# Column norms of the keys by full float32 matmuls on three column strips, keys turned on VectorE, in a hybrid RWKV-7 block

## The chip, the cores and the metric

The kernel runs on one core of a Trainium2 chip. The metric is the device time of one execution in microseconds (us). Engines are named as in the profile: PE is TensorE's matmul stream and PEld its weight loads, DVE is VectorE, ACT is ScalarE, POOL is GpSimd, and SP is the engine that issues the DMAs. Each of them works through its own queue of instructions in the order in which the program was built.

## The reference, cut to what matters

One layer of a language model with two branches that read the same normalised input (528 positions: 16 learned meta tokens and 512 of the sequence; model width 2048):

```python
P = hn @ w_in                          # 2048 -> 4*1024 + 64 + 64 + 4*1024 columns
r, k, v, g_r, wl, al = split(P[:RW])   # after a token shift
decay = exp(-exp(w_raw(wl)));  a = sigmoid(a0 + al @ a_lora_up)
kk = k * k_k;  kk = kk / max(norm(kk, per head of 64), 1e-12)
k  = k * (1 + (a - 1) * k_a)
# per head, step by step over the positions, in chunks of 64:
S = S * w_t - (S @ kk_t) (kk_t * a_t)^T + v_t k_t^T;   y_t = S @ r_t
y_a = (groupnorm(y) + bonus(r, k, v)) * silu(g_r)
y_b = Bg * causal_conv3(Cg * hc) * silu(g_c)          # the other branch
out = rmsnorm(h + concat(y_a, y_b) @ w_out)
```

What the change touches is the preparation of the recurrence: the squared norm of kk per head and position, and the two operands B (from kk * a) and K (from k) of the state's update, which the recurrence needs with the positions on the partitions.

## The kernel before

**Main stream.** The projection runs as one long stream of matmuls on PE. A tile is 128 output columns by 528 positions and takes 2048 rows of the weight as 16 steps of 128; the weight of a tile comes as four *quarters* (128 by 512, four of the 16 steps each), numbered 0 to 259 over the stream. Each product is done as three fp32r matmuls, high weight by high input, high weight by low input, low weight by high input (`steps`, L306 to L318; the matmul is L315). `prefetch` (L130 to L138) brings two quarters with one DMA `wr` on SP (L134). `split_w` (L123 to L128) then casts each quarter to its high half `wh` on ACT (L126) and subtracts to get the low half `wl` (L127), on DVE for even quarters and on POOL for odd ones. Six buffers of each are in use.

The stream visits the tiles in a fixed plan: k, r, v of the eight head pairs (two heads of 64 make one tile of 128), g (the gate), and C, h, B, gc of the other branch, by turns two pairs and one set C, h, B, gc; the last four sets come at the end. Pair 1 is in the first turn, pairs 2 and 3 in the second, and so on. When a tile is complete it is evacuated: L334 scales it from PSUM (for k, r, v, g, C, h, B, gc, each in two halves), L351 and L352 on ACT and DVE do the token shift of r and g, L362 belongs to the gate. For the other branch h is followed by a product on POOL (L401), a scaling on ACT (L403) and two steps of the convolution on DVE (L405).

**What stands between.** The preparation of a pair (`prepare`, from L569) is a function that issues its own instructions and, between them, calls `fill(ns)`, which lets the main stream issue for so many nanoseconds of counted PE time. The constants are in the table `FW` (L43 to L46). So the order of PE's queue is written by hand, by these fills. On the other engines a scheduler sets the order: it takes the instructions by priority and estimated readiness, with the weight splits 3000 and some evacuations 6000 ns ahead of the place at which they were issued (`WEIGHTS`, `AHEAD`). `later` (L482) puts a few steps on a clock of their own.

**The part changed,** per pair `i` in `prepare`:

- `sq` = (k * k_k) squared, on ACT (L615); split in high and low halves by `split` (L548 to L553: cast L551 on ACT, subtract L552 on DVE); `rk` (r times bonus factors) split likewise (L617).
- Gram blocks (`gram`, L623 to L630): for each chunk and each of the two heads one float32 matmul of 64 rows, 128 by 128. Eight chunks go in one cluster into four PSUM banks, then `masked` (L632) takes them to `gt` on DVE.
- fill gram2 (4800), then chunk 8's two Gram blocks in the banks misc and ser, and 16 transposes of B and K by PE (L655, an identity as the other operand) into two banks of the pool tz; ACT copies them to `bt` (L661).
- fill gram3 (3500), then `n2`: the norms as column sums. The weight is a column of ones for each head (`ones[:, P:P+2]`, 128 by 2), the moving operand is `sq`'s high and low half, in two pieces of 288 positions: four matmuls (L666, L667), two copies on ACT (L668). Then `zb`, two matmuls for the bonus (L670, L671) and a copy (L672).
- fill misc (2000). Then SP issues a block of DMAs: `sn` (the norms to DRAM, L685), `sg` (Gram blocks, L689), `ar` and `gt` to the operand store `opd` (L567), `d` and `nd` back (L697, L698) for the solve of 16 by 16 triangles on DVE (L701 to L734), four for `bt` (`stash`, L752 to L755), `rbd` (L758), eight for `vs` (v turned by DVE in 32 by 32 blocks, L762).

Later the inverses of pairs of preparations (`invert`, L772) and at the end the recurrence (`recur`, L875) run on PE. The recurrence loads 64 by 64 weights from the stored operands; its state update `zs` (L941) uses B and K.

Of the kernel before, what the change touches and what calls it, by code (L numbers as in the profile page):

```python
# [9 lines left out]
F32 = mybir.dt.float32  # L10
# [8 lines left out]
P = 128  # L19
# [21 lines left out]


FW = dict(  # L43
    evac=34, start=1062, lora=2200, gram=8000, gram_b=13500, gram2=4800, gram3=3500, misc=2000, v=2000, vt=1000, solve=22500, solve_first=26000,
    tr=3200, lev=3000, cp=4200, out=1500, begin=17000, p=2900, u=2900, s=5200, last=3700, mix=2600,
)  # L46

# [29 lines left out]
def hymba_kernel(ctx: ExitStack, tc: tile.TileContext, xt, xtok, w_in, w_out, pv, lup, cst, msk, gf, out):  # L77
# [84 lines left out]
    def tr(name, dt=F32):  # L162
        return cq.tile([P, LP], dt, tag="tr", name=name, bufs=5)
# [384 lines left out]
    def split(t, name, n):  # L548
        hi = tr(f"{name}_h", F32R)[:, 0:n]
        lo = tr(f"{name}_l", F32R)[:, 0:n]  # L550
        nc.scalar.copy(hi, t)  # L551
        nc.vector.tensor_tensor(out=lo, in0=t, in1=hi.bitcast(F32), op=ALU.subtract)  # L552
        return hi, lo  # L553
# [15 lines left out]
    def prepare(i):  # L569
# [43 lines left out]

        sq = tr(f"sq{i}")
        nc.scalar.activation(sq, k, AF.Square, scale=col(V_KK, i))  # L615
        sqh, sql = split(sq, f"sq{i}", LP)
        rh, rl = split(r, f"rk{i}", SEQ)  # L617
        fill(FW["gram_b" if p else "gram"])

        gt = cq.tile([P, 2, NCH, P], F32, tag=f"gt{p}", name=f"gt{i}")  # L620
        bt = cq.tile([P, 2, NCH - 1, CH], F32, tag="bt", name=f"bt{i}")

        def gram(z, c, c0):  # L623
            for h, hs, ho in heads:
# [7 lines left out]
        def masked(z, c0, c1):  # L632
            with ahead():
                for h in range(2):
                    nc.vector.tensor_tensor(
                        out=gt[:, h, c0:c1],
                        in0=z[h],
                        in1=gmask[:, h].unsqueeze(1).to_broadcast([P, c1 - c0, P]),
                        op=ALU.mult,
                    )  # L640
# [6 lines left out]
        masked(za, 0, 4)  # L647
        masked(zc, 4, 8)
        fill(FW["gram2"])
        ze = [pi.tile([P, 1, P], F32, tag=("misc", "ser")[h], name=f"g{i}_8_{h}") for h in range(2)]  # L650
        zz = [pz.tile([P, NCH - 1, CH], F32, tag="tz", name=f"bt{i}_{h}") for h in range(2)]
        gram(ze, 8, 8)
        for c in range(NCH - 1):
            for h, hs, ho in heads:
                nc.tensor.transpose(  # L655
                    zz[h][:, c], bk[hs, c, h : h + 2, :].rearrange("p a s -> p (a s)"),
                    ident[hs, 64 * h : 64 * h + 64],
                )
        masked(ze, 8, 9)
        for h in range(2):  # L660
            nc.scalar.copy(bt[:, h], zz[h])  # L661
        fill(FW["gram3"])
        n2 = tr(f"n2{i}")
        for j, (a, b) in enumerate(((0, 288), (288, LP))):
            z = pi.tile([2, b - a], F32, tag=("misc", "ser")[j], name=f"n2_{i}_{a}")
            nc.tensor.matmul(z, ones[:, P : P + 2], sqh[:, a:b], start=True, stop=False)  # L666
            nc.tensor.matmul(z, ones[:, P : P + 2], sql[:, a:b], start=False, stop=True)  # L667
            nc.scalar.copy(n2[0:2, a:b], z)  # L668
        zb = pz.tile([P, SEQ], F32, tag="tz", name=f"zb{i}")
        nc.tensor.matmul(zb, ones[:, 0:P], rh, start=True, stop=False)  # L670
        nc.tensor.matmul(zb, ones[:, 0:P], rl, start=False, stop=True)  # L671
        nc.scalar.copy(r, zb)  # L672
        fill(FW["misc"])

# [7 lines left out]
        def blocks(t):  # L682
            return bass.AP(tensor=t.tensor, offset=t.offset, ap=[[BLK, 8 * NCH], [CH, 16], [1, 16]])

        nc.sync.dma_start(  # L685
            bass.AP(tensor=sn.tensor, offset=sn.offset, ap=[[CH, 2], [P, NCH], [1, CH]]), c3(n2[0:2])
        )
        for h in range(2):
            nc.sync.dma_start(rows(sg, h), gt[64 * h : 64 * h + 64, h, :, 0:CH])  # L689
        NB = 8 * NCH  # L690
# [59 lines left out]
        later(16500 if p else 33000, load_inverse)  # L750

        for h, hs, ho in heads:  # L752
            stash(i, bt[hs, h], O_B, CH, 64 * h, 64, 0, NCH - 1)
            stash(i, bt[ho, h], O_K, CH, 64 * h, 64, 0, NCH - 1)
        until("v", i)  # L755
        v = got["v", i]
        nc.vector.tensor_tensor(out=r, in0=r, in1=v[:, CH:LP], op=ALU.mult)
# [117 lines left out]
    def recur(ch):  # L875
        ops = {}
        load_chunk(ch, 0, range(NPAIR), ops)
        load_chunk(ch, 1, range(NPAIR), ops)
        st = None
        for c in range(NCH):  # L880
            last = c == NCH - 1
            z = [pz.tile([P, 2, 4, CH], F32, tag="tz", name=f"rz{c}_{e}") for e in range(2)]
            for k in range(4):
                for part in range(0 if c else 1, 2):
                    for e in range(2):
                        t = ops[c, 2 * k + e]
                        o = O_KK if part else O_AR
                        for h, hs, ho in heads:
                            nc.tensor.matmul(  # L889
                                z[e][ho if e else hs, 0, k], t[hs, o : o + CH],  # L890
                                t[hs, O_V : O_V + CH] if part else st[hs, 4 * e + k],
                                start=(part == 0 or c == 0), stop=(part == 1),
                            )
            pn = ch.tile([P, 2, 4, CH], F32, tag="pn", name=f"pn{c}", bufs=2)
            with ahead():
                for e in range(2):
                    nc.scalar.activation(pn[:, e], z[e][:, 0], AF.Copy, scale=-1.0)
            if c and not last:
                load_chunk(ch, c + 1, range(0, 4), ops)
            fill(FW["p"])  # L900
            for k in range(4):
                for e in range(2):
                    t = ops[c, 2 * k + e]
                    for h, hs, ho in heads:
                        m = ho if e else hs
                        nc.tensor.matmul(z[e][hs, 1, k], t[m, O_X : O_X + CH], pn[m, e, k], start=True, stop=True)
            u = ch.tile([P, 2, 4, CH], F32, tag="u", name=f"u{c}", bufs=2)
            with ahead():
                nc.scalar.copy(u[:, 0], z[0][:, 1])
                nc.vector.tensor_copy(u[:, 1], z[1][:, 1])  # L910
            if c and not last:
                load_chunk(ch, c + 1, range(4, NPAIR), ops)
            fill(FW["u"])
            here, there = [], []
            if not last:
                zs = pi.tile([P, NPAIR, CH], F32, tag="misc", name=f"zs{c}")
            if c:
                zy = pi.tile([P, NPAIR - 1, CH], F32, tag="ser", name=f"zy{c}")
            for k in range(4):
                for e in range(2):  # L920
                    t, j = ops[c, 2 * k + e], 4 * e + k
                    if not last:
                        here += [(zs, j, t, O_B, u[:, e, k], 0, 2), (zs, j, t, O_K, t[:, O_V : O_V + CH], 1, 2)]
                    if c and j < NPAIR - 1:
                        there += [
                            (zy, j, st[:, j], O_AR + CH, t, 0, 3),
                            (zy, j, t[:, O_V : O_V + CH], O_KK + CH, t, 1, 3),
                            (zy, j, u[:, e, k], O_BR, t, 2, 3),
                        ]
                    elif c:  # L930

                        here += [
                            (z[0][:, 0], 0, t, O_AR + CH, st[:, j], 0, 3),
                            (z[0][:, 0], 0, t, O_KK + CH, t[:, O_V : O_V + CH], 1, 3),
                            (z[0][:, 0], 0, t, O_BR, u[:, e, k], 2, 3),
                        ]
            for n in range(max(len(here), len(there))):
                if n < len(here):
                    d, j, t, o, x, a, b = here[n]
                    for h, hs, ho in heads:  # L940
                        nc.tensor.matmul(d[hs, j], t[hs, o : o + CH], x[hs], start=(a == 0), stop=(a == b - 1))  # L941
                if n < len(there):
                    d, j, x, o, t, a, b = there[n]
                    for h, hs, ho in heads:
                        nc.tensor.matmul(d[ho, j], t[hs, o : o + CH], x[hs], start=(a == 0), stop=(a == b - 1))  # L945
            if not last:
                new = ch.tile([P, NPAIR, CH], F32, tag="st", name=f"st{c}", bufs=2)
                scale = dd[:, c].unsqueeze(2).to_broadcast([P, NPAIR, CH])
                with ahead():
                    if c:  # L950
                        nc.vector.tensor_tensor(out=new, in0=zs, in1=st, op=ALU.add)
                    nc.vector.tensor_tensor(out=new, in0=new if c else zs, in1=scale, op=ALU.mult)
                st = new
            if c:
                norm(ch, (zy, z[0][:, 0, 0:1]), c)
            fill(FW["s"])
# [278 lines left out]
```

## Time and profile before

| what | value |
|---|---|
| median of 3 runs | 1056.57 us (1055.68 to 1056.75) |
| the profiled execution | 1055.68 us, of it the span 1053.9 us |
| granted TensorE clock | 0.996 |
| PE busy | 1035.8 us, 98% of the span |
| PEld, DVE, ACT, POOL busy | 90%, 54%, 35%, 29% |
| one projection matmul, 258 or 512 columns, start to start | 0.12 us, 0.23 us |
| `wl` on DVE, alone | 0.69 us |
| `wh` on ACT | 0.62 us |
| 32 by 32 transposes of 128x512 on DVE (L785) | 0.70 us |

How to read it. The page's first part gives each engine's busy time and its share of the span; the chain is followed back from the last instruction to what released each step. The timeline lists instructions by start, with the duration as modelled; as matmuls overlap, the distance from one start to the next says more about PE than a duration does. In brackets stands how long the engine had been idle, and what ended that. The list of waits gives the total, the number and the longest.

### The profile page before, as it was taken

The page shows a single profiled execution, that of the slowest core. Times are in us where ns is not written, and L with a number is a line of the kernel's source. Part 1 is how long each engine was busy: PE and PEld are TensorE (multiplying, and loading weights), DVE is VectorE, ACT ScalarE, POOL GpSimd, SP SyncE. Part 2 cuts the span into 40 slices and gives each one's busy share as a digit, 9 for nine tenths or more (in the row PEclk, how much of TensorE's full clock was granted, in tenths as well). Part 3 has the DMA queues.
Part 4 walks back from the last instruction along what each step waited for, and adds up shares of the span by engine and source line. Part 5 has one row for each costly group of instructions (what it writes and reads, how often), then busy time and mean ns, then how long its engine had stood idle before and what let it go on. Part 6 is the DMA issues. An engine that isn't in the chain of part 4 may idle for free.

```text
span 1053.9 us, 23986 instructions
## 1 busy us (share of the span) xinstructions
PE 1035.8 (98%) x9973; PEld 945.8 (90%) x9973; DVE 565.4 (54%) x1072; ACT 366.3 (35%) x682; POOL 307.8 (29%) x315
## 2 busy tenths in 40 slices
PE   7999999999999999999999999999999999999996
PEld 6999998999998999989999989888898988888885
DVE  6774965559563658653757642455454771212132
ACT  7553422433332433233443232222222432323232
POOL 0132413324222323132323231323233242424232
PEclk9999999999999999999999999999999999999999
DMA  8446475364843363753364648777644978323314
GB/s 295 137 121 158 117 177 142 108 154 119 207 141 114 109 161 116 175 155 114 104 170 129 169 134 288 233 216 247 184 144 110 280 225 305 98 85 98 100 61 160
DMA packets 182893, 167.49 MB, mean 159 GB/s; under 512 B 120960, under 2 KB 143232, under 8 KB 182400
## 3 DMA queue, kind: packets, MB, share of 16 engines
q1 hardware_dynamic: 182208, 164.90, 54.0%
q8 instruction: 78, 1.28, 0.5%
q10 hardware_dynamic: 576, 1.07, 0.3%
q14 instruction: 31, 0.25, 0.1%
HBM read 129.05 MB, written 36.88 MB: 157 GB/s over the span
## 4 chain that ended last, share of the span: by engine, by line
PE 91%; DVE 4%; issue 2%; DMA 1%; ACT 1%; POOL 1%; SPq 0%; DVEq 0%; ACTq 0%; POOLq 0%
PE o L1070 17%; PE ps_g L315 9%; PE ps_C L315 9%; PE ps_gc L315 9%; PE ps_k L315 9%; PE ps_B L315 8%; PE ps_h L315 8%; PE ps_r L315 7%; PE ps_v L315 7%; PE g L625 2%; PE zs L941 1%; PE rz L889 1%; PE ps_lora L315 1%; PE zy L945 1%; DMA wq<-in_w_in_dram 1%
## 5 line engine op out<-in xcount | busy, mean ns | idle before, releaser
L127 POOL TENSOR_TENSOR wl<-wr,wh 128x512 fp32r<-128x512 f32 x150 | 210.4, 1405 | 458.0 <-ACT wh L126 428.0
L126 ACT CAST wh<-wr 128x512 fp32r<-128x512 f32 x312 | 188.8, 619 | 390.0 <-PE o L1070 93.6
L127 DVE TENSOR_TENSOR wl<-wr,wh 128x512 fp32r<-128x512 f32 x162 | 124.4, 773 | 244.0 <-ACT wh L126 243.6
L1070 PE MATMUL o<-wh,m 128*128 128x512 f32 (+1 forms) x484 | 145.3, 384 | 0.0
L1070 PEld LDWEIGHTS o<-wh,m 128*128 128x128 f32 x484 | 89.6, 188 | 21.3
L1070 PE MATMUL o<-wl,m 128*128 128x512 f32 (+1 forms) x242 | 92.6, 389 | 0.0
L315 PE MATMUL ps_k<-xl,wh 128*128 128x264 f32 x256 | 73.1, 286 | 0.0
L315 PE MATMUL ps_v<-xh,wh 128*128 128x264 f32 x256 | 73.1, 286 | 0.0
L315 PE MATMUL ps_g<-xh,wl 128*128 128x258 f32 (+1 forms) x256 | 72.2, 282 | 0.9 <-DVE wl L127 0.8
L315 PE MATMUL ps_r<-xh,wh 128*128 128x258 f32 (+1 forms) x256 | 72.2, 282 | 0.8 <-ACT wh L225 0.8
L315 PE MATMUL ps_k<-xh,wh 128*128 128x264 f32 x256 | 73.0, 285 | 0.0
L315 PE MATMUL ps_h<-xh,wl 128*128 128x258 f32 (+1 forms) x256 | 72.8, 284 | 0.0
L315 PE MATMUL ps_k<-xh,wl 128*128 128x264 f32 x256 | 72.7, 284 | 0.0
L315 PE MATMUL ps_v<-xh,wl 128*128 128x264 f32 x256 | 72.7, 284 | 0.0
L315 PE MATMUL ps_v<-xl,wh 128*128 128x264 f32 x256 | 72.7, 284 | 0.0
L315 PE MATMUL ps_g<-xl,wh 128*128 128x258 f32 (+1 forms) x256 | 72.5, 283 | 0.0
L315 PE MATMUL ps_h<-xh,wh 128*128 128x258 f32 (+1 forms) x256 | 72.3, 282 | 0.0
L315 PE MATMUL ps_C<-xh,wh 128*128 128x258 f32 (+1 forms) x256 | 72.3, 282 | 0.0
L315 PE MATMUL ps_g<-xh,wh 128*128 128x258 f32 (+1 forms) x256 | 72.3, 282 | 0.0
L315 PE MATMUL ps_C<-xh,wl 128*128 128x258 f32 (+1 forms) x256 | 72.3, 282 | 0.0
L315 PE MATMUL ps_h<-xl,wh 128*128 128x258 f32 (+1 forms) x256 | 72.2, 282 | 0.0
L315 PE MATMUL ps_r<-xl,wh 128*128 128x258 f32 (+1 forms) x256 | 72.1, 282 | 0.0
(271 smaller groups left out, 2706.3 us busy)
## 6 DMA issues: line engine op xcount, KB each, us to landing
wr<-in_w_in_dram SPq DMA_DIRECT2D x127, 512.0 KB
ct<-opd SPq DMA_DIRECT2D x64, 288.0 KB
wr<-in_w_out_dram SPq DMA_DIRECT2D x32, 512.0 KB
opd<-ar SPq DMA_DIRECT2D x8, 576.0 KB
opd<-gt SPq DMA_DIRECT2D x16, 288.0 KB
opd<-bt SPq DMA_DIRECT2D x32, 128.0 KB
xres<-in_xtok_dram SPq DMA_DIRECT2D x4, 768.0 KB
out_dram<-xres SPq DMA_DIRECT2D x6, 512.0 KB
```

Of the source, the lines that this page charges most:

```text
L126: nc.scalar.copy(hi, rq)
L127: eng.tensor_tensor(out=lo, in0=rq, in1=hi.bitcast(F32), op=ALU.subtract)
L315: nc.tensor.matmul(ps[r], ww[:, w], xx[:, kt, a:b], start=(kt == 0 and n == 0), stop=(kt == KT - 1 and n == 2))
L625: nc.tensor.matmul(z[h][:, c - c0], bk[hs, c, h : h + 2, :].rearrange("p a s -> p (a s)"), ar[hs, c].rearrange("p a s -> p (a s)"), start= ...
L889: nc.tensor.matmul(z[e][ho if e else hs, 0, k], t[hs, o : o + CH], t[hs, O_V : O_V + CH] if part else st[hs, 4 * e + k], start=(part == 0 ...
L941: nc.tensor.matmul(d[hs, j], t[hs, o : o + CH], x[hs], start=(a == 0), stop=(a == b - 1))
L945: nc.tensor.matmul(d[ho, j], t[hs, o : o + CH], x[hs], start=(a == 0), stop=(a == b - 1))
L1070: nc.tensor.matmul(ps[t + p], mm[:, tk], ww[:, o], start=(jj == 0 and q == 0), stop=(jj == KT - 1 and q == 2))
```

## The change

1. The keys are turned on DVE. `bt` becomes a tile of [128, 8, 2, 32, 2], and two DVE transposes (each 128x512, in blocks of 32 by 32) fill it straight from `bk`, before the Gram blocks. PE's 16 transposes and ACT's two copies go. As blocks of 32 by 32 are turned where they stand, the rows of `bt` go out in eight DMAs (32 partitions, 8 chunks, 64 elements) and not in four. In `opd` B and K then lie interleaved, element by element, and the recurrence takes its 64 by 64 weights with a stride of two elements.
2. The norms are one full float32 product each, with no split of `sq`: three matmuls of 192 positions, with 32 columns of the block of ones (16 of each head) as the weight, on the column strips 0, 32 and 64 of the array and into one PSUM bank of [96, 192]. One copy takes them out; `sn` goes out in two DMAs.
3. Chunk 8's Gram blocks go to banks of the pool tz, and directly behind them, in one cluster, come the norms and `zb` (now in the bank ser). The fill gram3 (3500) is gone, gram2 is 5500. The masks of chunk 8 and the copy of the norms are issued with the priority `AHEAD`.

The diff (line numbers in the text above are those of the kernel before):

```diff
-    ... gram=8000, gram_b=13500, gram2=4800, gram3=3500, misc=2000, ...
+    ... gram=8000, gram_b=13500, gram2=5500, misc=2000, ...
@@ prepare
-        sqh, sql = split(sq, f"sq{i}", LP)
         rh, rl = split(r, f"rk{i}", SEQ)
         fill(FW["gram_b" if p else "gram"])
-        bt = cq.tile([P, 2, NCH - 1, CH], F32, tag="bt", name=f"bt{i}")
+        bt = cq.tile([P, NCH - 1, 2, CH // 2, 2], F32, tag="bt", name=f"bt{i}")
+        for a in range(2):
+            nc.vector.transpose(bt[:, :, :, :, a], bk[:, 0 : NCH - 1, a].rearrange("p c (t s) -> p c t s", t=2))
...
         fill(FW["gram2"])
-        ze = [pi.tile([P, 1, P], F32, tag=("misc", "ser")[h], name=f"g{i}_8_{h}") for h in range(2)]
-        zz = [pz.tile([P, NCH - 1, CH], F32, tag="tz", name=f"bt{i}_{h}") for h in range(2)]
+        ze = [pz.tile([P, 1, P], F32, tag="tz", name=f"g{i}_8_{h}") for h in range(2)]
         gram(ze, 8, 8)
-        for c in range(NCH - 1):
-            for h, hs, ho in heads:
-                nc.tensor.transpose(
-                    zz[h][:, c], bk[hs, c, h : h + 2, :].rearrange("p a s -> p (a s)"),
-                    ident[hs, 64 * h : 64 * h + 64],
-                )
-        masked(ze, 8, 9)
-        for h in range(2):
-            nc.scalar.copy(bt[:, h], zz[h])
-        fill(FW["gram3"])
-        n2 = tr(f"n2{i}")
-        for j, (a, b) in enumerate(((0, 288), (288, LP))):
-            z = pi.tile([2, b - a], F32, tag=("misc", "ser")[j], name=f"n2_{i}_{a}")
-            nc.tensor.matmul(z, ones[:, P : P + 2], sqh[:, a:b], start=True, stop=False)
-            nc.tensor.matmul(z, ones[:, P : P + 2], sql[:, a:b], start=False, stop=True)
-            nc.scalar.copy(n2[0:2, a:b], z)
-        zb = pz.tile([P, SEQ], F32, tag="tz", name=f"zb{i}")
+        z = pi.tile([96, 192], F32, tag="misc", name=f"n2_{i}")
+        for g in range(3):
+            nc.tensor.matmul(
+                z[32 * g : 32 * g + 32], ones[:, 48:80].bitcast(F32), sq[:, 192 * g : 192 * g + 192],
+                start=True, stop=True,
+            )
+        zb = pi.tile([P, SEQ], F32, tag="ser", name=f"zb{i}")
         nc.tensor.matmul(zb, ones[:, 0:P], rh, start=True, stop=False)
         nc.tensor.matmul(zb, ones[:, 0:P], rl, start=False, stop=True)
+        n2 = tr(f"n2{i}")[0:96, 0:192]
+        with ahead():
+            nc.scalar.copy(n2, z)
+            masked(ze, 8, 9)
         nc.scalar.copy(r, zb)
         fill(FW["misc"])
...
-        nc.sync.dma_start(
-            bass.AP(tensor=sn.tensor, offset=sn.offset, ap=[[CH, 2], [P, NCH], [1, CH]]), c3(n2[0:2])
-        )
+        for h in range(2):
+            nc.sync.dma_start(
+                bass.AP(tensor=sn.tensor, offset=sn.offset + CH * h, ap=[[3 * P, 3], [P, 3], [1, CH]]),
+                n2[16 - 16 * h : 96 - 16 * h : 32].rearrange("p (c s) -> p c s", s=CH),
+            )
...
         for h, hs, ho in heads:
-            stash(i, bt[hs, h], O_B, CH, 64 * h, 64, 0, NCH - 1)
-            stash(i, bt[ho, h], O_K, CH, 64 * h, 64, 0, NCH - 1)
+            for b in range(2):
+                for t in range(2):
+                    stash(
+                        i, bt[64 * h + 32 * b : 64 * h + 32 * b + 32, :, t].rearrange("p c s a -> p c (s a)"),
+                        O_B + 64 * b, 64, 64 * h + 32 * t, 32, 0, NCH - 1,
+                    )
@@ recur
-    here += [(zs, j, t, O_B, u[:, e, k], 0, 2), (zs, j, t, O_K, t[:, O_V : O_V + CH], 1, 2)]
+    bb = t[:, O_B : O_B + 2 * CH].rearrange("p (s a) -> p a s", a=2)
+    here += [(zs, j, bb[:, 0], 0, u[:, e, k], 0, 2), (zs, j, bb[:, 1], 0, t[:, O_V : O_V + CH], 1, 2)]
...
-    nc.tensor.matmul(d[hs, j], t[hs, o : o + CH], x[hs], start=(a == 0), stop=(a == b - 1))
+    w = t[hs, o : o + CH] if o else t[hs]
+    nc.tensor.matmul(d[hs, j], w, x[hs], start=(a == 0), stop=(a == b - 1))
```

More of the change, by code (lines that the diff above doesn't have):

```diff
@@ L43 @@
 FW = dict(
-    evac=34, start=1062, lora=2200, gram=8000, gram_b=13500, gram2=4800, gram3=3500, misc=2000, v=2000, vt=1000, solve=22500, solve_first=26000,
+    evac=34, start=1062, lora=2200, gram=8000, gram_b=13500, gram2=5500, misc=2000, v=2000, vt=1000, solve=22500, solve_first=26000,
     tr=3200, lev=3000, cp=4200, out=1500, begin=17000, p=2900, u=2900, s=5200, last=3700, mix=2600,
```

## The prediction

> **What bounds the kernel now.** I read the page's first part, then the chain that ended last.
>
> ```profile
> PE 1035.8 (98%) x9973; PEld 945.8 (90%) x9973; DVE 565.4 (54%) x1072; ACT 366.3 (35%) x682; POOL 307.8 (29%) x315
> ...
> PE 91%; DVE 4%; issue 2%; DMA 1%; ACT 1%; POOL 1%; SPq 0%; DVEq 0%; ACTq 0%; POOLq 0%
> ```
>
> TensorE (PE) is busy 98% of the span and carries 91% of the chain. So an edit is worth what it takes from TensorE's own queue, plus the waits in that queue that it makes or ends. Work on VectorE (DVE), ScalarE (ACT), GpSimd (POOL) or the DMA issuer (SP) costs nothing while TensorE does not wait for it. Next I read TensorE's waits:
>
> ```profile
> PE ps_B L315 <- DVE wl L127: 0.9, 1, 0.9
> ...
> PE ps_g L315 <- DVE wl L127: 0.8, 2, 0.4
> ```
>
> Columns: total us, times, longest. There are few (the longest are two of 1.6 and 1.3 for "issue" in the recurrence), and the regular ones are for wl, the low half of a weight quarter, which L127 makes shortly before use. That is the thing to watch: the weight splits stand in the same in-order queues as the changed steps.
>
> **Part 1, the clusters.** Each pair interrupts the projection stream three times (L642, L651, L664). The timeline of TensorE for pair 0, last two clusters:
>
> ```profile
> 82.57 0.28 PE L315 MATMUL ps_r<-xh,wh 128*128 128x258 f32 x1
> 82.79 0.49 PE L625 MATMUL g<-ar,bk 64*128 64x128 f32 x4
> 83.11 0.66 PE L655 MATMUL bt<-cs,bk 64*128 64x64 f32 x16
> 83.70 0.38 PE L315 MATMUL ps_r<-xl,wh 128*128 128x258 f32 x1
> 83.92 0.28 PE L315 MATMUL ps_r<-xh,wl 128*128 128x258 f32 x1
> ...
> 87.59 0.29 PE L666 MATMUL n<-sq_h,ones 128*2 128x288 f32 x1
> ...
> 88.12 0.40 PE L670 MATMUL zb<-rk_h,ones 128*128 128x512 f32 x1
> ...
> 88.59 0.28 PE L315 MATMUL ps_r<-xh,wh 128*128 128x256 f32 x1
> ```
>
> Starts follow each other by 0.12 in the stream. From 82.57 to 83.92 is 1.35; less two normal steps, the Gram and transpose cluster costs 1.11: entry 0.10, g 0.32, bt 0.59, exit 0.10. The norms' cluster costs 0.53 for n (87.59 to 88.12) and 0.47 for zb (to 88.59): 1.00. Together 2.11 per pair.
>
> After: entry 0.10, g 0.32, the switch from row halves to column strips 0.10 (as the other switches), n, a switch back 0.10, zb 0.47. A full float32 matmul shows as two passes; g's two passes of 128 columns take 0.11 each in the row above (0.32 with the fill), so 192 columns take 0.16 a pass and 0.32 both. Strips side by side: n 0.32; one after another: 0.96. The strips' first weight load is not hidden behind another tile's stream; the weight-load rows are 0.10 for 32 columns and 0.19 for 128, I take 0.16. Sum 1.57, or 2.21 for strips in sequence. No row of before has strips in one bank; the nearest are the 64x64 tiles of the inverse, four of which come out in 0.06 where one such stream of 64 columns is 0.05, so tiles do run side by side, and I take 1.57. **Eight pairs: 8 x (1.57 - 2.11) = -4.3**; in sequence +0.8.
>
> [...]
>
> The Gram block of the last chunk moves from the banks misc and ser to the pool tz. In pairs 3 and 5 its cluster starts 0.33 and 0.43 late (266.97 and 420.14 in the timeline), while the masks still read misc and ser. That goes: **-0.8**.
>
> **Part 2, work off TensorE.** Per pair the change removes on ACT one cast (0.67), two bt copies (0.59 each), two n copies (0.38 each), adds one n copy (some 0.3); on DVE it removes sq_l (0.75) and adds two 32x32-block transposes (0.70 each, the L785 row's duration); on SP it adds five DMA issues (8 of 0.5 to 0.64 for bt instead of 4 of 0.64, and 2 for sn). By itself all this is hidden. Its cover is the lead of the weight splits, so the question is where those stand afterwards.
>
> **Part 3, the order.** Queues run in order, and the order is fixed when the program is built, so I compared both builds. The block of DMAs on SP (sg, gt, sn, d, nd, bt, rbd, vs; some 14 us of issue) comes earlier, as its norms do by the 3500 ns fill that is gone, and passes a weight DMA per pair (wr22, wr43, wr67, wr91 among them). Casts and subtractions of those weights move back on ACT and DVE too. I took each quarter whose wl now stands behind an operation that itself waits for a recent projection, and set its finish against its first use. Three kinds have no slack.
>
> (a) Quarter 44, start of ps_B0 in pair 1. Its cast now stands behind L403, its wl behind L334 and L405. All engines in that stretch:
>
> ```profile
> 154.26 1.29 POOL L401 TENSOR_TENSOR u<-u,hh 128x514 f32<-128x514 f32 x1 [11.02 <-DVE hh L334]
> ...
> 155.59 0.72 ACT L403 ACTIVATE cv<-u,pvt 128x512 f32<-128x512 f32 x1 [13.70 <-POOL u L401]
> ...
> 156.35 1.54 DVE L405 SCALAR_TENSOR_TENSOR cv<-u,pvt,cv 128x512 f32<-128x512 f32 x2 [2.17 <-ACT cv L403]
> ```
>
> This is a chain: hh (second half 153.78 to 154.19), POOL, ACT, DVE twice, 157.89 at its end; then wl, 0.69 alone, 1.77 for the one of before that ran here beside POOL's. So wl44 is ready at 158.6 to 159.6, or 0.9 sooner if the solve ahead of hh ends earlier (157.7); its use is at 153.00 (third row of ps_B in TensorE's timeline). The wait is 4.7 to 6.6; I take 5.3. It contains the wait of quarter 46 (start 158.33 to 159.63, 1.08 above a normal step), which sat behind the same chain two quarters later and goes. Net **+4.2** (3.6 to 5.5).
>
> (b) Quarters 74, 122, 170 (middle of ps_v, pairs 3, 5, 7). wl now waits for ACT L351 and DVE L352 of the same pair's r; pr_r's second half ends at 249.32, L351 at 250.08, L352 (0.74) at 250.8, wl (0.68) at 251.5, and 0.6 sooner without the solve's operations between; the use is at 250.46: 0.4 to 1.1, three times 0.75. The waits two quarters later (0.55, 0.55, 0.27) go. Net **+0.9** (-0.2 to +1.9).
>
> (c) Quarters 86, 134, 182 (middle of ps_C1, C2, C3). In before wl86 stood ahead of the 16x16 solve; now it stands behind both evacuations of ps_g3 and nearly the whole solve (L700 to its first 72x512 product). Two rows of before on DVE:
>
> ```profile
> 284.66 0.16 DVE L709 TENSOR_TENSOR y<-tt,nd 72x8 f32<-72x8 f32 x1
> ...
> 291.03 1.05 DVE L719 TENSOR_TENSOR prod<-d,y 72x512 f32<-72x512 f32 x1
> ```
>
> L709 to the end of that product is 292.08 - 284.66 = 7.4 without a gap; the four operations ahead of L709, which now start only behind pr_g's second half (284.32 to 284.7), are 0.9. So wl starts at 293.0 and ends at 293.7. Quarter 86 is first needed low at 290.07. The wait is 3.6, three times **+10.8**. Less if the solve's small operations run faster alone (nothing shows that), more by 1 if POOL's subtraction runs beside wl: 3.0 to 4.6 each.
>
> Further quarters (30 to 37 in pair 1, 88, 90, 138, 186) keep 0.4 us or more of slack by the same sums.
>
> **Part 4, the recurrence.** Its 256 matmuls with B or K (L941) now load weights with a stride of two elements. No weight load of before is strided. Bounds: free, as contiguous ones; or doubled, 0.053 for 64 columns, 256 x 0.053 = 13.6 if nothing hides it, a quarter of that if the four tiles share it. The nearest rows, contiguous 64-column loads, are hidden beside streams, so I take 0. [...] The 1.6 (L941) and 1.3 (L945) waits for "issue" may stay or go; 0 here, 1.5 to either side.
>
> **Sum.** -4.3 - 0.8 + 4.2 + 0.9 + 10.8 = **+10.8**. The profiled run is 1055.68 (span 1053.9 and 1.8 around it), so 1066.5 for it; the median is 0.9 above the profiled run, so 1067.4. TensorE's clock is 0.996; I leave it.
>
> **Rivals.**
> - *Plain gain.* The moved splits are in time after all, because an order in a queue is no time. Then part 1 remains (-5.1), and the four waits of before may go (-2.5): 1049 to 1051.5. It decides if wl86 ends before 290, so if the solve starts 3.6 before ps_g3 ends; against it, L334 of ps_g3 stands ahead in the same queue. For it: TensorE waited only 2.5 in all for wl in before. Chance 0.20.
> - *Half the waits.* (c) comes to 1 or 2 each: 1059 to 1062, or only (a) is there: 1056.5. Chance 0.10.
> - *Strided loads slow.* 3.4 to 13.6 on top: 1071 to 1081. Chance 0.10.
> - *Strips in sequence.* 5.1 on top: 1072.5. Against: the strips use different columns of the array; for: all three write one bank, which no row shows. Chance 0.08.
>
> **How the numbers follow.** The forecast has 0.52, its own range by the bounds above 1061 to 1073. To hold 8 in 10 the range takes in half of the plain gain and the cheaper half of the slow loads: 1050 to 1074. About 0.2% (2.1 us) is what a measurement can tell from no change: faster holds the plain gain and a little of the second rival, 0.22; same 0.08; slower 0.70.
>
> **What would show it.** Right: TensorE waits "ps_B <- wl" near 5 once and "ps_C <- wl" near 3.6 three times; no waits at quarters 46 and 76; 1.6 from stream to stream around one cluster less two steps. Wrong: TensorE without those waits (plain gain); the cluster near 2.2 (strips in sequence); L945's B and K tiles 0.05 further apart (strided loads). If the waits are there but another quarter has them, the size is wrong and not the mechanism.

## The result and the profile after

The changed kernel takes 1073.99 us (median of 4 runs, 1071.13 to 1074.85) against 1056.12 (4 runs, 1055.27 to 1056.75): a ratio of 1.0163, interval 1.0144 to 1.0181. That is 17.9 us slower, where 10.8 were forecast. The profiled execution took 1074.71, of it the span 1072.9, 19.0 above the span before. The granted clock fell from 0.996 to 0.987. Against the 1067.4 us of the forecast it is 6.6 more.

From the changed kernel's page, the busy times and the chain:

```profile
PE 1040.6 (97%) x9861; PEld 949.0 (88%) x9861; DVE 567.1 (53%) x1080; ACT 351.8 (33%) x650; POOL 320.2 (30%) x315
...
PE 91%; DVE 3%; issue 2%; DMA 2%; SPq 0%; POOL 0%; ACT 0%; DVEq 0%; ACTq 0%; POOLq 0%
```

Its list of TensorE's waits (total us, times, longest):

```profile
PE ps_C L315 <- DVE wl L127: 11.7, 3, 4.1
PE ps_B L315 <- ACT wh L126: 3.1, 1, 3.1
PE ps_B L315 <- DVE wl L127: 2.0, 1, 2.0
...
PE g L628 <- DVE gt L638: 0.7, 1, 0.7
```

PE has 112 matmul records fewer than before and is yet busy 5 us longer: some of its work ran slower. The waits are the new thing, 16.8 us for weight halves where there were 1.7.

The merged cluster of pair 0, in TensorE's timeline:

```profile
83.52 0.28 PE L315 MATMUL ps_r<-xh,wh 128*128 128x258 f32 x1
83.73 0.49 PE L628 MATMUL g<-ar,bk 64*128 64x128 f32 x4
84.15 0.53 PE L658 MATMUL n<-sq,ones 128*32 128x192 f32 x6
84.61 0.50 PE L663 MATMUL zb<-rk_h,ones 128*128 128x512 f32 x1
...
85.18 0.28 PE L315 MATMUL ps_r<-xl,wh 128*128 128x258 f32 x1
85.30 0.28 PE L315 MATMUL ps_r<-xh,wl 128*128 128x258 f32 x1
```

From 83.52 to 85.30 is 1.78; less two steps of 0.12 the cluster costs 1.54, where 1.57 was worked out. From the first start of the three strips (two passes each) to that of zb it is 0.46, where 0.48 was worked out with the weight load; in sequence the passes alone would be 0.96. So the strips run side by side.

What the merged cluster does to the queues is seen at quarter 86. First SP, where the DMA wr43, which brings quarters 86 and 87, now stands behind most of the block (wr43 is the 41st at L134, as the first three have lines of their own); in the kernel before it was issued at 261.96:

```profile
274.49 3.08 SPq L567 DMA_DIRECT2D opd<-bt  x6
...
288.48 0.38 SPq L134 DMA_DIRECT2D wr<-in_w_in_dram  x1
```

Then VectorE and TensorE:

```profile
298.15 1.02 DVE L718 TENSOR_TENSOR prod<-d,y 72x512 f32<-72x512 f32 x1
299.08 0.68 DVE L127 TENSOR_TENSOR wl<-wr,wh 128x512 fp32r<-128x512 f32 x1
```

```profile
295.59 0.28 PE L315 MATMUL ps_C<-xl,wh 128*128 128x258 f32 x1
299.82 0.39 PE L315 MATMUL ps_C<-xh,wl 128*128 128x258 f32 x1 [3.95 <-DVE wl L127]
...
300.99 0.34 PE L315 MATMUL ps_C<-xh,wl 128*128 128x258 f32 x1
301.13 0.41 PE L315 MATMUL ps_C<-xh,wh 128*128 128x256 f32 x1
301.34 0.41 PE L315 MATMUL ps_C<-xl,wh 128*128 128x256 f32 x1
```

The split stands behind the solve's first 72x512 product and ends at 299.76; the matmul that needs it starts at 299.82, after 3.95 idle. Then comes what the forecast left out: the first steps are 0.12, but from 301.13 on they are 0.21, for 3.5 us. The windows show it as the granted clock (the last three numbers of a line are clock, DMA share, GB/s):

```profile
295.00:299.80 4.80, 0.87 (x8) 0.67 (x6) 4.35 (x16) 1.14 (x2) 1.30 (x1) 1.00 0.67 244
299.80:301.10 1.30, 1.28 (x10) 1.28 (x11) 1.26 (x2) 0.00 (x0) 1.11 (x1) 0.99 0.28 28
301.10:304.60 3.50, 3.50 (x19) 3.50 (x18) 2.73 (x4) 0.64 (x2) 0.00 (x0) 0.52 0.68 178
304.60:309.00 4.40, 4.40 (x39) 4.40 (x38) 2.32 (x4) 2.16 (x4) 2.80 (x3) 1.00 0.31 113
```

The clock is 1.00 while TensorE waits and 0.99 in the 1.3 us after, 0.52 for 3.5 us (half clock from here on), then 1.00 again: 19 matmuls in 3.5 us, and then 39 in 4.4.

At quarter 44 the wait has two parts, first for the cast and then for the split:

```profile
156.73 0.50 PE L315 MATMUL ps_B<-xh,wh 128*128 128x512 f32 x1 [3.12 <-ACT wh L126]
...
159.48 0.80 PE L315 MATMUL ps_B<-xh,wl 128*128 128x512 f32 x1 [2.02 <-DVE wl L127]
```

Where the 19 us went, by the start of the same stream matmul in both traces (after minus before, stage by stage, "by starts" below; rounded, so the rows add up to 19.1):

| stretch | change in us | of it |
|---|---|---|
| start and pair 0 | -0.1 | |
| pair 1, to its C | +1.0 | wait for the masks, less the cluster |
| quarter 44 (ps_B0) | +6.9 | waits +5.5, slow clock +2.4, quarter 46 -1.0 |
| pairs 2 and 3 | -2.1 | clusters -1.1, masks -0.3, quarter 76 -0.7 |
| quarter 86 (ps_C1) | +5.7 | wait +4.0, slow clock +1.7 |
| pairs 4 and 5 | -2.2 | clusters -1.1, masks -0.4, quarter 124 -0.7 |
| quarter 134 (ps_C2) | +6.3 | wait +3.8, slow clock +2.5 |
| pairs 6 and 7 | -1.5 | clusters -1.1, quarter 172 -0.4 |
| quarter 182 (ps_C3) | +5.8 | wait +4.1, slow clock +1.7 |
| recurrence and tail | -0.7 | waits for "issue" come and go |

### The profile page after: what moved, and what is told of

Its sections match the earlier page's. It is cut to its first block, busy times and chain, and to the rows that moved or that the text cites. A ratio compares the mean times of both kernels' runs of the same rounds, so it can differ in the third digit from the quotient of the medians.

```text
span 1072.9 us, 23783 instructions
## 1 busy us (share of the span) xinstructions
PE 1040.6 (97%) x9861; PEld 949.0 (88%) x9861; DVE 567.1 (53%) x1080; ACT 351.8 (33%) x650; POOL 320.2 (30%) x315
## 4 chain that ended last, share of the span: by engine, by line
PE 91%; DVE 3%; issue 2%; DMA 2%; SPq 0%; POOL 0%; ACT 0%; DVEq 0%; ACTq 0%; POOLq 0%
PE o L1075 17%; PE ps_v L315 9%; PE ps_B L315 9%; PE ps_gc L315 9%; PE ps_k L315 8%; PE ps_g L315 8%; PE ps_r L315 8%; PE ps_h L315 8%; PE ps_C L315 6%; PE g L628 2%; DMA wq<-in_w_in_dram 1%; PE zs L946 1%; PE zy L950 1%; PE ps_lora L315 1%; PE rz L892 1%
## 5 line engine op out<-in xcount | busy, mean ns | idle before, releaser
L127 POOL TENSOR_TENSOR wl<-wr,wh 128x512 fp32r<-128x512 f32 x150 | 224.1, 1497 | 468.1 <-ACT wh L126 447.3
L315 PE MATMUL ps_C<-xh,wl 128*128 128x258 f32 (+1 forms) x256 | 74.8, 292 | 11.7 <-DVE wl L127 11.7
L315 PE MATMUL ps_C<-xh,wh 128*128 128x258 f32 (+1 forms) x256 | 75.0, 293 | 0.0
L315 PE MATMUL ps_C<-xl,wh 128*128 128x258 f32 (+1 forms) x256 | 74.7, 292 | 0.0
L315 PE MATMUL ps_r<-xh,wl 128*128 128x258 f32 (+1 forms) x256 | 72.3, 282 | 0.0
```

The lines of the kernel that those rows point to most:

```text
L127: eng.tensor_tensor(out=lo, in0=rq, in1=hi.bitcast(F32), op=ALU.subtract)
L315: nc.tensor.matmul(ps[r], ww[:, w], xx[:, kt, a:b], start=(kt == 0 and n == 0), stop=(kt == KT - 1 and n == 2))
```

## The experiments

The theory after the result: the new operations cost nothing and the clusters gain; the loss is that the weights' splits stand later in the in-order queues (17.4 us of waits, by starts) and that TensorE runs at half clock, 0.50 to 0.52, for some microseconds at each of the four places (8.3 us). Rivals: the new operations cost (strided loads, strips, more DMAs); the early norms by themselves cost; the slow stretch has a cause of its own.

**1 and 2. The weights' DMAs first.** In the changed kernel (e1) and in the kernel before (e2):

```diff
-            state["dma"] = nc.sync.dma_start(raw, stream[j]).ins
+            with tc.high_priority(offset=WEIGHTS):
+                state["dma"] = nc.sync.dma_start(raw, stream[j]).ins
```

> The changed kernel, with one more thing: the DMA of a weight (wr, L134) gets the same priority as the splits that use it, so that it and the splits stand ahead of the block of descriptor DMAs again; TensorE's own order is the same as in the changed kernel. Order theory (the loss is the four waits for late splits, 17.2 us in all, and the slow clock behind each): no wait for wl or wh above 0.5 us is left, the clock is back at 0.995, and what remains is the clusters' gain of 0.65 in each of eight pairs, the 2.4 us of waits that the kernel before has, perhaps less 1.7 in pair 1: 1047 to 1052 us. Rival theory (the new operations cost by themselves: strided weights, strips in one bank, more and smaller DMAs): it stays above 1065 us.

> The kernel before with the same priority for the DMA of a weight. Order theory: it has little to repair here, the waits for wl at quarters 46, 76, 124 and 172 (2.4 us together): 1053 to 1056 us, and the difference to the changed kernel with the same priority is the pure worth of the new clusters, 4 to 6 us. Rival: if the priority by itself gains more than 5 us here, then the repair in the other run is not a repair of what the change did.

Measured: 1128.35 (ratio 1.0688, 1.0673 to 1.0702) and 1110.21 (1.0502, 1.0469 to 1.0535). Both were missed widely. The waits at ps_B0 and ps_C are gone, but others came, one of 3.4 us for a split on POOL among them. The waits of e1, first TensorE's, then SP's queue:

```profile
PE t L796 <- DVE xn L789: 42.0, 4, 11.9
...
PE g L629 <- DVE gt L639: 4.6, 4, 2.0
PE ps_g L316 <- POOL wl L127: 3.4, 1, 3.4
```

```profile
SPq L135 <- POOL wl L127: 346.1, 117, 7.7
SPq L135 <- DVE wl L127: 181.1, 81, 10.4
```

A weight's DMA waits until an older weight has been split and its buffer is free; standing first, it holds up all behind it on SP: these waits total 527 us, in the changed kernel 433 (249.2 and 183.5), in the kernel before 402 (258.4 and 143.5). So the Gram blocks, the solve and the inverse's operand come late, and TensorE waits 42 us at the inverse (L796). The edit repaired one order by breaking the opposite one. It made the kernel before 54 us slower as well, so e1's time, though above the 1065 set for the rival, decides nothing between the theories. It shows that the order on SP has two sides.

**3. The merge undone** (e3):

```diff
-    ... gram2=5500, misc=2000, ...
+    ... gram2=4800, gram3=3500, misc=2000, ...
         gram(ze, 8, 8)
+        with ahead():
+            masked(ze, 8, 9)
+        fill(FW["gram3"])
...
             nc.scalar.copy(n2, z)
-            masked(ze, 8, 9)
```

> The changed kernel with the merge undone: chunk 8's Gram blocks after a fill of 4800, then a fill of 3500, then the norms and zb, as in the kernel before; transposes on VectorE, strips, eight DMAs and strided weights stay. In the built order quarters 44, 86, 134 and 182 stand ahead again, 74, 122 and 170 stay behind ScalarE's L351. Order theory: no waits of 3 us and more, clock 0.99 or better; the clusters gain less, since one more entry and exit (0.2 to 0.3) is paid in each pair: 1050 to 1056 us. Rival (the new operations cost): above 1065 us.

Measured: 1050.31 (ratio 0.9949, 0.9936 to 0.9961), clock 0.996, as the order theory said. Transposes on VectorE, strips, eight DMAs and strided weights are all in it, and it is faster than the kernel before by 6 (1056.33 beside it): the rival of costly new operations falls.

**4 and 12. The waits filled with work.** e4 fills the three waits at ps_C, e12 those at ps_B0 too. The weight `zero` is a tile of zeros, so the sums stay as they were (the lines that make it are left out here, and the column range is shortened to `a:b`):

```diff
+            if k4 == 0 and name == "B0":          # e12 only
+                for _ in range(24):
+                    nc.tensor.matmul(ps[0], zero, xh[:, 0, a:b], start=True, stop=True)
+            if k4 == 2 and name in ("C1", "C2", "C3"):
+                for _ in range(33):
+                    nc.tensor.matmul(ps[0], zero, xh[:, 0, a:b], start=False, stop=False)
             yield from steps(ps, ranges, k4, 4 * j + k4)
```

> The changed kernel with 33 more matmuls of 258 columns with a weight of zeros, 0.12 us each, ahead of the third weight quarter in each of ps_C1, ps_C2 and ps_C3, which add nothing to the sums; all else stands in the same order. They fill the three waits of 3.8 to 4.1 us with work. Clock theory (TensorE runs at half clock for a while because it had stood idle): the three waits shrink to 0.3 or less, the starts behind them stay 0.12 apart, the granted clock rises from 0.987 to 0.993 or more, and the time falls by 5 to 6.5 us against the changed kernel, to 1067 to 1069, though TensorE does 12 us more work. Rival (the slow stretch comes from what else runs there, not from the idle time): the slow stretches stay and the time stays at 1073 to 1075.

> The run with the filled waits again, and 24 more matmuls of 512 columns with a weight of zeros ahead of ps_B of pair 1 as well (0.23 us each, 5.5 us, the sum of the two waits there); all else in the same order. In the changed kernel the slow stretches behind the four places cost 2.4, 1.7, 2.5 and 1.7 us by the starts of the stream. Clock theory: none is left, the granted clock is 0.995 or better in every run, and against the changed kernel (1074.0, ratio 1.0163) the median falls by 6 to 8.5 us: 1065.5 to 1068, ratio 1.0085 to 1.012, clear of the noise of some 2 us that the recurrence's waits make, though TensorE has 17.5 us more to do. Rival (the slow stretch is not from the idle time): ratio 1.014 or more.

Measured: e4 1071.87 (ratio 1.0158, 1.0142 to 1.0175), 3 above the upper end expected and not clear of the changed kernel. Stage by stage it is clear, in the profiled execution, which was the fastest of the four (1069.76): its stream gains 1.4, 2.1 and 1.8 us on the changed kernel's at the three places, 5.3 together, and the clock there is 1.00; another 2.3 came in pair 1, ahead of the filled places, and the recurrence, with 2.8 us of waits for "issue" in this trace (1.2 in the changed kernel's), gave 2.2 back. So e12 was made, with more at stake: 1066.31 (1.0084, 1.0070 to 1.0099), 7.7 below the changed kernel, clock 0.997 in its profile. In e12's windows, across the place at quarter 86 and behind it:

```profile
292.00:297.00 5.00, 4.81 (x41) 4.61 (x39) 4.66 (x13) 1.14 (x2) 1.34 (x2) 1.00 0.65 247
297.00:301.00 4.00, 4.00 (x36) 4.00 (x35) 3.71 (x6) 0.28 (x1) 0.62 (x1) 1.00 0.61 149
301.00:305.00 4.00, 4.00 (x36) 4.00 (x35) 3.01 (x4) 2.43 (x5) 2.54 (x3) 1.00 0.48 134
```

TensorE had 17 us more to do and the kernel became faster. The clock is 1.00 in these windows and in those from 150 to 165, at quarter 44, where the changed kernel shows 0.62 from 156 to 165: with the idle time filled the slow stretches are gone, so here they come from it. Not all of the gain is theirs. By starts the profiled span is 7.4 shorter: the four places give 6.8, pair 1's wait for the masks, which the added matmuls do not touch, 1.1, and the recurrence takes 0.6 back.

**5, 6, 9, 10. One constant.** The fill ahead of the merged cluster, all else as in the changed kernel:

```diff
-    ... gram2=5500, ...
+    ... gram2=6500, ...      # e5; 8300 in e6, 5800 in e9, 7000 in e10
```

> The changed kernel with one constant changed: the fill ahead of the merged cluster is 6500 in place of 5500, so the cluster comes some 1 us of stream later. In the built order quarters 44, 86, 134 and 182 then stand ahead of the L405 steps and of the solve again; 74, 122 and 170 still stand behind L352 on VectorE. Order theory (the loss is where the splits stand, not what the new operations cost): the waits of 3 us and more and the slow stretches go, clock 0.995 or better, 1047 to 1052 us, and some 1 us below the run with two clusters (1050.3) for the entries and exits saved. Rival (early norms or the merged cluster itself cost, the order only goes along with them): a loss that shrinks by the 1 us of the shift, so 1065 us or more.

> The changed kernel with the fill at 8300, which is the sum of the two fills of the kernel before: one cluster, where the norms stood before. In the built order no quarter but 46 stands close behind a late projection. Order theory: 1046 to 1051 us, no wait above 1.5 us; pair 1's wait for the masks (0.7 and 0.2 in the changed kernel) goes too, since they have 2.8 us more. The later solve could move other waits: then the loss is at the inverses (L795), not at weights.

> The changed kernel with the fill ahead of the merged cluster at 5800 in place of 5500: 0.3 us of stream. In the built order quarters 44, 86, 134 and 182 already stand in front. If the loss hangs on that order alone, this is as good as the run at 6500 (1046.7): 1046 to 1050 us, no wait above 2 us. If it hangs on how early the norms come, it is nearly as bad as the changed kernel: above 1068 us.

> The changed kernel with that fill at 7000. In the built order more of pair 1's solve stands between hh and the split of quarter 46 than at 6500 (8 operations against 4; at 8300, with 21, that quarter waited 4.4 us). So: one wait at ps_B of 1.5 to 2.5 us, with no slow clock behind it, 1047 to 1049 us. If the 8300 run lost its 5.7 us to something else than this wait and the clock behind it, 7000 lies halfway between, near 1049 to 1050, without that wait.

| fill | median us | ratio and interval | TensorE's longest wait for a weight |
|---|---|---|---|
| 5500 | 1073.99 | 1.0163 (1.0144 to 1.0181) | 4.1, three times near 4 |
| 5800 | 1049.60 | 0.9920 (0.9891 to 0.9949) | 1.1 |
| 6500 | 1046.69 | 0.9908 (0.9893 to 0.9924) | 1.3 |
| 7000 | 1049.15 | 0.9917 (0.9892 to 0.9942) | 0.5 |
| 8300 | 1052.39 | 0.9964 (0.9952 to 0.9977) | 4.4 |

0.3 us of fill is worth 24 us. Nothing else differs, so the loss hangs on the order that the fill decides, and not on early norms. The order is seen on SP in the run at 5800, where wr43 stands ahead of the block:

```profile
266.27 0.54 SPq L134 DMA_DIRECT2D wr<-in_w_in_dram  x1
266.85 2.06 SPq L567 DMA_DIRECT2D opd<-bt  x4
```

The run at 6500 is the best version found, 9.8 below its kernel before and 0.3 below the range expected. At 8300 the expectation missed the wait of 4.4, and its range by 1.4: the later solve of pair 1 (its 72x512 operations run from 158.04 to 161.59) stands ahead of quarter 46's split. VectorE and TensorE of e6:

```profile
161.51 1.28 DVE L127 TENSOR_TENSOR wl<-wr,wh 128x512 fp32r<-128x512 f32 x2
```

```profile
162.24 0.79 PE L315 MATMUL ps_B<-xh,wl 128*128 128x512 f32 x1 [4.41 <-DVE wl L127]
162.83 0.63 PE L315 MATMUL ps_B<-xh,wh 128*128 128x512 f32 x1
```

The next matmul of 512 columns is already at the longer duration (0.63 for 0.39), which the changed kernel's have at a clock of 0.50 (160.07 to 164.34). Of the 6.0 us between the profiled spans at 6500 and 8300, 4.4 arise at this place by starts. At 7000 the wait that was expected at ps_B came to 0.5, and 1.7 appeared at the inverse (L795). The time, 1049.15, is that of the alternative in the expectation (near 1049 to 1050, without that wait), so this run does not support the reading of the one at 8300; the stages do.

**7 and 8. Half of the bt DMAs on another queue.** Four of the eight bt DMAs of a pair from ScalarE's queue, with the fill at 5500 (e7) and at 8300 (e8):

```diff
-        nc.sync.dma_start(spot(...), src)
+        (nc.scalar if act else nc.sync).dma_start(spot(...), src)     # act=(b == 1) for bt
```

> The changed kernel with four of the eight bt DMAs of each pair issued from ScalarE's queue in place of SP's; fills and all else as in the changed kernel. In the built order the weights' DMAs and splits then stand ahead again (all but 46 of pair 1). Order theory, in its narrow form (the four more issues on SP push the weight DMAs back): the waits of 3 us and more go, 1047 to 1053 us. Rival (it is the early norms that pull the block ahead, whatever its length): the waits stay and the time is 1065 us or more. The issues may cost ScalarE 0.5 us each, which delays its casts; then waits for wh appear.

> Both repairs, the fill at 8300 and half of the bt DMAs from ScalarE's queue. Order theory: within 1.5 us of the better one of the two, since each already puts the splits in front; 1046 to 1051 us. If it is slower than both by more than 2 us, a third thing depends on the place of the norms' cluster.

Measured: e7 1055.45 (0.9989, 0.9979 to 0.9999), with no wait above 1.0 for a weight. With the early norms left as they are, four issues off SP take 18 us away, and wr43 is issued at 269.26, where it was 288.48: that supports the narrow form, that the longer block on SP pushes the weights' DMAs back. The range was missed by 2.5. Two groups of waits of TensorE in e7:

```profile
PE ps_h L315 <- DVE wl L127: 2.6, 3, 1.0
PE ta L521 <- ACT tz L526: 2.5, 3, 0.8
```

The second is ScalarE come late; against the run at 5800, which has no such wait, it costs 3.2 by starts, over pairs 3, 5 and 7. The first stands in the run at 5800 too (2.2, three times), so ScalarE's queue does not explain it. What the rest of the 6 us between these two runs is stays open.

e8 was expected within 1.5 of the better one and was slower than both, 1067.41 (1.0102, 1.0088 to 1.0116): 11.0 us of waits at the inverse for its transposed operand (L795), four times, up to 4.4, and clock 0.988. Why these came only with both repairs was not settled.

**11. Early norms alone** (e11): the kernel before with

```diff
-    ... gram3=3500, ...
+    ... gram3=700, ...
```

> The kernel before with the fill between chunk 8's cluster and the norms at 700 in place of 3500: the norms and the block of DMAs come as early as in the changed kernel, with none of its new operations and with four bt DMAs. In the built order the late quarters are those of the kernel before. Order theory: about the time of the kernel before, 1053 to 1058 us, no wait of 3 us. If early norms alone cost, 1065 us or more.

Measured: 1058.83 (1.0010, 0.9994 to 1.0027), 0.8 above the range expected, with the kernel before at 1057.24 beside it; no wait above 1.4. Early norms with four bt DMAs cost nothing measurable; late norms with eight (e3) gain; early with eight lose 18 at a fill of 5500 and gain at 5800. So neither alone makes the loss, and both together make it only where the order tips.

## Why the prediction was right, and where it was not

- **What bounds it, and the direction: right.** TensorE's queue is the bound and the late weight splits decide. The quarters that waited are those named, 44, 86, 134 and 182.
- **The number: inside the range by luck.** 1073.99 is 0.01 below the upper end, and two of the four executions (1074.71 and 1074.85) lie above it. That end was set by the cheaper half of the slow strided loads, which cost nothing here; the forecast alone reached to 1073. What took the time there is the clock, below.
- **Clusters, -4.3 and -0.8: right per pair, wrong in pair 1.** Pairs 2 to 7 gained 3.4 in clusters (0.57 each, 0.54 worked out) and 0.7 in bank waits. In pair 1 the Gram block, now in the pool tz, waited for VectorE's masks instead (g from gt 0.7, zb from gt 0.2): that stretch lost 1.0 and not gained 0.5. One bank wait went, another came.
- **(a) +4.2: right.** By starts the waits were 5.5 (5.3 worked out), net of quarter 46 4.5. The chain ran as written, but TensorE waited first for the cast (3.1) and then for the split (2.0), where one wait of near 5 for wl was named. The L405 steps ended at 157.74 in a stream that stood 0.9 later than before's, so at the early end of the range, and the split beside POOL's took some 1.8, the late end of its own.
- **(b) +0.9: wrong sign.** Quarters 74, 122, 170 did not wait; the waits two quarters later went (-1.8). From the end of pr_r's second half to the end of wl it took 2.2, as worked out (254.35 to 256.51). But the use came at 257.70, 3.35 behind pr_r, where the row of before gave 1.14 (249.32 to 250.46): VectorE's steps were 5.0 later than before's and the stream 7.2. Why VectorE was sooner in the stream was not tested.
- **(c) +10.8: right, a little small.** 4.0, 3.8 and 4.1 for 3.6 each, 11.9. One operation of the solve (L727 at 293.77) took 1.19 instead of 0.17.
- **"TensorE's clock is 0.996; I leave it": the step that failed.** The page of before gave the clock of a kernel that never waits long; the forecast put waits of 4 to 5 us into it and kept its clock. At these places the half clock cost 8.3 us, three quarters of the forecast's whole sum. Filled with work (e12), the kernel comes to 1066.31; the sum had 1067.4. That it comes so near is in part chance, as the misses in pair 1, (b) and (c) offset each other.
- **The rivals.** Strided loads: free; a group of 160 records of the recurrence takes 2.61 us in both kernels, and the weight loads' mean is 135 to 136 ns for 134 to 135. Strips in sequence: 0.46 says no. The plain gain is what happens when the order holds: 1046.69 at a fill of 6500, below the 1049 to 1051.5 set for it; its recurrence is 1.8 shorter by starts, where the forecast put 0, 1.5 to either side.

## What to carry to other kernels

When a change shortens an engine's work but moves when its results appear, compare the order of every queue before counting the gain: here four more DMA issues on one queue and 0.3 us of fill decided between a gain of 8 us (at 5800) and a loss of 18. In a kernel that TensorE bounds, price a wait of several microseconds (3.7 to 4.1 here, 5.1 in two parts at quarter 44) at its length plus the slow clock that goes with it (1.7 to 2.5 us each here). And move the consumer (one fill constant) before forcing a priority: with the weights' DMAs put first, SP's queue stood 527 us for their buffers (e1; 433 in the changed kernel), and TensorE waited 42 us at the inverse.

## What the runs showed of the hardware

Windows laid at the edges of the slow stretches of the changed kernel show a clock of 0.50 from 157.71 to 164.54, 301.07 to 304.49, 454.67 to 461.50 and 615.10 to 618.51, so for 6.83 or 3.41 us, and 1.00 between them. TensorE worked 5.1, 3.4, 5.1 and 3.4 us in the four, and half of that, 8.5, is near the 8.3 by starts.

In this kernel the idle times of TensorE above 1.1 us, after the first 30 us, are those at the four places: 3.12 and 2.02 at quarter 44, then 3.95, 3.71 and 4.06. At quarter 134 the half clock began during the wait, 1.71 before the work resumed; at quarter 44 it began 0.98 after the first wait, inside the second, and at the other two 1.25 and 1.12 after the work resumed. Waits of 3 us and more stand beside a lower mean clock in e1 (up to 11.9; 0.967), e2 (up to 6.7; 0.975), e8 (up to 4.4; 0.988) and e4 (3.1; 0.993); the profiles of e3, e5, e7, e9, e10, e11 and e12, without such a wait, show 0.995 to 0.997. e6, with its one wait of 4.4, shows 0.995 too.

Shorter waits show that the length of one wait does not decide. Idle times of 1.33 (quarter 46 in the run at 6500, where the clock is 1.00 from 156 to 165) and 1.63 (L941 in the kernel before, 1.00 from 725 to 740) left the clock alone; but 1.34 in e11 and 1.69 in e10 were followed by 0.50. TensorE and a window of e11:

```profile
127.05 0.97 PE L625 MATMUL g<-ar,bk 64*128 64x128 f32 x3 [1.34 <-DVE gt L635]
```

```profile
128.00:130.00 2.00, 2.00 (x21) 1.88 (x18) 0.59 (x3) 1.02 (x2) 0.19 (x2) 0.50 0.86 226
```

The windows of e10, where the 1.7 stood between two groups of 64x64 matmuls:

```profile
167.00:170.00 3.00, 1.31 (x65) 1.11 (x64) 1.70 (x3) 0.19 (x1) 2.49 (x2) 1.00 0.78 224
170.00:172.00 2.00, 2.00 (x16) 1.56 (x7) 0.69 (x1) 1.93 (x4) 0.00 (x0) 0.68 0.82 295
172.00:174.00 2.00, 2.00 (x7) 1.52 (x6) 0.00 (x0) 0.18 (x1) 1.28 (x1) 0.50 0.04 12
```

What else decides was not shown.
